# Scores of the samples' paged keys: half of the pages as one product on VectorE and sums on ScalarE

## The chip, the cores and the metric

The kernel runs on one core of a Trainium2 chip. The metric is device time in microseconds, the median of several executions. The engines named below are PE (TensorE, matrix products), VectorE (DVE), ScalarE (ACT), GpSimd (POOL) and SyncE (SP), whose queue issues the transfers (DMA). "The profile" is one recorded execution.

## The reference

One inference step of a decoder trunk with two layers, for a prompt of 512 tokens and 8 samples of one token each. Layer 0 runs a convolution module and a stick-breaking attention of 8 heads of width 128 side by side behind one input projection; layer 1 is a gated DeltaNet. All is fp32. The change touches one thing, the logits of a sample's query against its past of 2048 keys, which lie in 16 pages of 128 keys (drawn by `page_table` from a pool of 160 pages):

```python
k_past = cache_k[j][page_table].reshape(n_seq, past_len, SB_HEADS, SB_HEAD_DIM)
z = jnp.einsum('bqhd,bkhd->bhqk', q.astype(F32), k.astype(F32)) * (SB_HEAD_DIM ** -0.5)
z = z + bias.astype(F32)[None, :, None, None]
```

From z follow softplus, a reversed cumulative sum over the keys, the weights, and their sum over the pages of values.

## The kernel before, in words

Tokens lie on the free dimension (512 + 8 = 520 columns), features on the 128 partitions. A projection takes a weight block of 8 x 128 x 128 from HBM (`weights`), ScalarE casts it to a high part `wh`, VectorE subtracts to get the low part `wl`, and PE adds three products of high and low parts into a PSUM tile `pg` (`products`); `wr` has three buffers, `wh` and `wl` two each.

Layer 0 goes over the 8 heads. Head h has the projections of convolution group h (`conv_gemm`), of k and v, and of two gates; then 31 taps of the depthwise convolution on one accumulator tile `acc` (`conv_taps`; the first on ScalarE, 30 on VectorE), a group norm (`conv_norm`, whose result is stored to HBM), the work of the samples, and the prompt's attention (`prompt_attention`, with exponentials and logarithms on ScalarE). The samples' work is spread over the heads: `scores(b)` of samples 0 and 1 at head 0, of 2, 3, then 4 and 5 at head 3, then 6 at head 4 and 7 at head 5, and `mix(b - 1)`, which multiplies the pages of values, beside them.

`scores(b)` copies the sample's query, spread over all partitions, to `qbc` (128 x 8 heads x 128). For each of the 16 pages it loads the page of keys (128 keys x 8 heads x 128, 512 KB) into a tile `page` (`page`, line 838 on); there are five such slots, which pages of values and other tiles use too. For each head one VectorE instruction multiplies the page's 128 columns by `qbc` and sums them into one column of z (`accum_out`), which the hardware runs as the product and a read of the accumulator.

Nothing runs in the order of the program's text. Each operation is recorded (`record`) with an engine, a cost, and a priority, its place in the text plus a bias; `flush` plans all of layer 0 as a list schedule with these costs, and each engine then gets its instructions in the planned order, which it keeps. Weight blocks have a bias far ahead of all, the matrix products one far behind, and `scores` and `mix` stand 2000 places ahead. By the written costs a score product takes 1.04 x 128 + 68 + 12 = 213 ns on VectorE, a product of 1024 columns 1.04 x 1024 + 68 = 1133 ns, and an accumulating ScalarE copy of 128 columns 0.83 x 128 + 109 + 105 = 320 ns. As every operation is issued from one helper, the profile gives line 431 for nearly all; groups are told apart by their tiles.

Of the kernel before, what the change touches and what calls it, by code (L numbers as in the profile page):

```python
# [11 lines left out]
AF = mybir.ActivationFunctionType  # L12
ALU = mybir.AluOpType
# [11 lines left out]
H = 8  # L25
# [471 lines left out]
def build(tc, a, ctx):  # L497
    nc = tc.nc
    sc = Sched(tc)
    V, S, G, PE, Q = (sc.engine(e) for e in ("DVE", "ACT", "POOL", "PE", "SP"))  # L500
# [17 lines left out]
    def C(name, p=P):  # L518
        o, n = COFF[name]
        t, lo, _ = next(x for x in tabs if x[1] <= o < x[2])  # L520
        return t[:p, o - lo:o - lo + n]
# [149 lines left out]
    with ExitStack() as l0:  # L671
# [165 lines left out]
        def page(b, p, cache):  # L837
            kt = pgp.tile([P, H, P], F32, name="page")
            sel = ptab[0:1, b * NPG + p:b * NPG + p + 1]

            def load():
                r = nc.sync.value_load(sel, min_val=0, max_val=NPOOL - 1)
                nc.sync.dma_start(kt, cache[bass.ds(r, 1)].rearrange("o p h d -> (o p) h d"))
            sc.record("SP", "page", load, (), {}, out=[kt], ins=[sel], cost=(340, 4 * P * P * H))
            return kt

        def scores(b):

            qbc = lp.tile([P, H, P], F32, name="qbc", bufs=1)
            for g in range(2):  # L850
                qp = pm.tile([P, 4, P], F32, name="pd", bufs=1)
                PE.matmul(qp.rearrange("p j d -> p (j d)"), sel8[:, b:b + 1].broadcast_to([P, P]),
                          qrow[:, g * 4:g * 4 + 4, :].rearrange("p j d -> p (j d)"), start=True, stop=True)
                S.copy(qbc[:, g * 4:g * 4 + 4, :], qp)
            z = lp.tile([P, H, NPG], F32, name="dz", bufs=2)
            for p in range(NPG):
                kt = page(b, p, a["cache_k"])
                for h in range(H):
                    junk = lp.tile([P, P], F32, name="junk", bufs=4)
                    V.scalar_tensor_tensor(junk, kt[:, h, :], 1.0, qbc[:, h, :], op0=ALU.mult, op1=ALU.mult,  # L860
                                           accum_out=z[:, h, p:p + 1])
            V.scalar_tensor_tensor(z, z, ISQ, sbb[:, :, None].broadcast_to([P, H, NPG]), op0=ALU.mult, op1=ALU.add)
            e = lp.tile([P, H, NPG], F32, name="de")
            w = lp.tile([P, H, NPG], F32, name="dw")
            S.activation(e, z, AF.Abs)
            S.activation(e, e, AF.Exp, scale=-1.0)
            V.tensor_scalar(w, e, 1.0, None, op0=ALU.add)
            V.scalar_tensor_tensor(e, w, 1.0, e, op0=ALU.subtract, op1=ALU.subtract)
            S.activation(w, w, AF.Ln)
            V.tensor_tensor(w, w, e, op=ALU.subtract)  # L870
            V.scalar_tensor_tensor(w, z, 0.0, w, op0=ALU.max, op1=ALU.add)
            wf = w.rearrange("p h g -> p (h g)")
            p1 = pm.tile([P, 2, P], F32, name="pd", bufs=1)
            PE.matmul(p1[:, 0, :], C("tri"), wf, start=True, stop=True)
            PE.matmul(p1[:, 1, :], ones, wf, start=True, stop=True)
            tot = lp.tile([P, H, NPG + 1], F32, name="dtot")
            V.memset(tot[:, :, NPG:], 0.0)
            V.tensor_copy(tot[:, :, 0:NPG], p1[:, 1, :].rearrange("p (h g) -> p h g", h=H))
            suf = lp.tile([P, H, NPG + 1], F32, name="dsuf")
            V.tensor_tensor_scan(suf.rearrange("p h g -> p (h g)")[:, ::-1], C("scan_dec")[:, ::-1],  # L880
                                 tot.rearrange("p h g -> p (h g)")[:, ::-1], 0.0, op0=ALU.mult, op1=ALU.add)
            V.tensor_tensor(z, z, suf[:, :, 1:], op=ALU.subtract)
            V.tensor_tensor(z, z, p1[:, 0, :].rearrange("p (h g) -> p h g", h=H), op=ALU.subtract)
            return z
# [26 lines left out]
        def head_gemm(h):  # L911
            ps = gemm1(8 + 3 * h)
            kt = lp.tile([P, NT], F32, name="kq", bufs=2)
            S.copy(_pn(kt), ps)
            Q.dma_start(a["o_k"][h], kt)
            ps = gemm1(8 + 3 * h + 1)
            vt = lp.tile([P, NT], F32, name="vt", bufs=2)
            S.copy(_pn(vt), ps)
            Q.dma_start(a["o_v"][h], vt)
            return kt, vt  # L920
# [65 lines left out]
        for h in range(H):  # L986
            with sc.prio(-HP):
                gp, win = conv_gemm(h)
                kt, vt = head_gemm(h)
                az, gate = gates_gemm(h)  # L990
            acc = conv_taps(h, gp, win)
            conv_norm(h, acc, az)
            with sc.prio(-2000):
                for b in ((0, 1), (2,), (3,), (4, 5), (6,), (7,), (8,), ())[h]:
                    z_next = scores(b) if b < NB else None
                    if b:
                        mix(b - 1, z_last)
                    z_last = z_next
            prompt_attention(h, kt, vt, gate)
            if h in (2, 3, 5, 6):  # L1000
                ada(0, 8 + (2, 3, 5, 6).index(h), lp)
# [119 lines left out]
    with ExitStack() as es:  # L1121
        op = sc.pool(es, "out0", 2)
# [699 lines left out]
    with ExitStack() as es:  # L1822
        op = sc.pool(es, "out1", 2)
# [117 lines left out]
```

## Time and profile before

| | |
|---|---|
| median of 3 runs | 3222.65 us (3216.93 to 3229.28) |
| profiled execution | 3229.8 us, span 3228.0 us |
| PE busy | 3072.7 us, 95% |
| VectorE busy | 2346.4 us, 73% |
| ScalarE busy | 1578.2 us, 49% |
| GpSimd busy | 128.3 us, 4% |
| mean granted clock of TensorE | 0.965 |

Busy times are sums over the span of an engine's records. Matmuls are pipelined and their ends are modelled, so a busy PE is not PE at its peak; records of VectorE and ScalarE overlap those of the next instruction, so the distance between starts is the better price of one. A wait is put down to the releaser that came last.

### The profile page before, as it was taken

What the parts mean: (1) busy time and instruction counts of PE and PEld (TensorE: products, weight loads), DVE (VectorE), ACT (ScalarE), POOL (GpSimd) and SP (SyncE); (2) the same over time, 40 slices, a digit from 0 to 9 for tenths busy, and PEclk for the clock granted to TensorE, in tenths of its full rate; (3) what the DMA queues carried; (4) which work ended last, traced back from release to release, by engine and by line L of the source; (5) the groups of instructions that cost most, each with busy time, mean ns of one, the idle gap of its engine ahead of it and who ended that gap; (6) DMA issues with size and microseconds to landing.
All of it is one profiled execution on the core that took longest, in us unless ns stands there. A gap on an engine that the chain in (4) does not pass through costs nothing.

```text
span 3228.0 us, 65519 instructions
## 1 busy us (share of the span) xinstructions
PE 3072.7 (95%) x24448; PEld 2800.0 (87%) x24448; DVE 2346.4 (73%) x6470; ACT 1578.2 (49%) x2942; POOL 128.3 (4%) x157
## 2 busy tenths in 40 slices
PE   8999999998979999999999979999999989999997
PEld 5798888886868886998999969999989779989997
DVE  3477988789674476676999749999956566665755
ACT  3234344433543366777773236555535555554544
POOL 0000000000001111000000000000000000001111
PEclk9999999999979999999999989999989789899998
DMA  9988898989627798687664485555364444476754
GB/s 316 296 274 292 298 313 293 327 306 316 219 89 260 287 308 276 141 168 149 151 155 135 110 153 176 154 150 168 127 180 146 137 126 154 130 247 193 227 181 137
DMA packets 361586, 667.01 MB, mean 207 GB/s; under 512 B 103698, under 2 KB 216339, under 8 KB 357171
## 3 DMA queue, kind: packets, MB, share of 16 engines
q1 hardware_dynamic: 361266, 662.82, 67.4%
q8 instruction: 192, 3.15, 0.4%
q14 instruction: 128, 1.04, 0.1%
HBM read 574.95 MB, written 87.70 MB: 205 GB/s over the span
## 4 chain that ended last, share of the span: by engine, by line
PE 84%; DVE 7%; DMA 6%; ACT 1%; SPq 1%; issue 1%; POOLq 0%; ACTq 0%; POOL 0%; DVEq 0%
PE pg L431 66%; PE pm L431 9%; PE pl L431 6%; PE pd L431 2%; SPq L431 1%; DVE wl L431 1%; DVE junk L431 1%; DMA S<-state_delta 1%; DMA page<-cache_k 1%; DMA wa<-w_ada 1%; DVE blk L431 1%; DVE acc L431 1%; DVE S L431 1%; DMA o_ds<-S 1%; DMA m<-sp 0%
## 5 line engine op out<-in xcount | busy, mean ns | idle before, releaser
L431 PE MATMUL pg<-uh,wh 128*128 128x260 f32 (+1 forms) x6112 | 1343.3, 290 | 12.5 <-ACT wh L431 6.2
L431 PE MATMUL pg<-ul,wh 128*128 128x260 f32 (+1 forms) x6112 | 1344.0, 289 | 3.0 <-DVE ul L431 2.6
L431 PEld LDWEIGHTS pg<-uh,wh 128*128 128x128 f32 (+1 forms) x6112 | 1001.0, 191 | 67.1 <-issue 46.0
L431 PEld LDWEIGHTS pg<-ul,wh 128*128 128x128 f32 (+1 forms) x6112 | 1004.0, 191 | 46.0 <-issue 33.8
L431 ACT CAST wh<-wr 128x1024 fp32r<-128x1024 f32 (+3 forms) x508 | 512.5, 1010 | 769.0 <-PE pg L431 634.2
L431 PE MATMUL pg<-uh,wl 128*128 128x260 f32 (+1 forms) x6112 | 880.6, 287 | 0.2
L431 DVE TENSOR_TENSOR wl<-wr,wh 128x1024 fp32r<-128x1024 f32 (+3 forms) x508 | 616.0, 1213 | 328.1 <-ACT wh L431 145.6
L431 PEld LDWEIGHTS pg<-uh,wl 128*128 128x128 f32 (+1 forms) x6112 | 791.6, 190 | 42.4 <-issue 37.3
L431 DVE SCALAR_TENSOR_TENSOR junk<-page,qbc 128x128 f32<-128x128 f32 x1024 | 223.2, 293 | 7.7 <-DMA page<-cache_k 4.4
L431 DVE TENSOR_TENSOR tmp<-m 128x224 f32<-128x224 f32 (+19 forms) x238 | 200.8, 844 | 4.0
L431 DVE SCALAR_TENSOR_TENSOR acc<-gp,conv_w_a,acc 128x512 f32<-128x512 f32 x240 | 181.5, 756 | 4.1 <-ACT acc L431 1.1
L431 ACT ACT_TABLE_LOAD x123 | 157.8, 1283 | 22.5 <-DVE rs L431 10.9
L431 DVE SCALAR_TENSOR_TENSOR cacc<-buf,conv_w_c,cacc 128x512 f32<-128x512 f32 x192 | 143.2, 746 | 13.8 <-ACT cacc L431 12.0
L431 DVE TENSOR_REDUCE m<-tmp 128x32 f32<-128x224 f32 (+19 forms) x238 | 131.1, 551 | 4.0
L431 DVE DVE_READ_ACCUMULATOR junk<-page,qbc 128x1 f32 x1024 | 90.2, 88 | 0.0
L431 PE MATMUL pl<-page,wst 128*32 128x512 f32 x512 | 80.2, 611 | 8.8 <-DMA page<-cache_v 8.8
L431 PE MATMUL pl<-wa,cpad 128*32 128x512 f32 x512 | 82.9, 604 | 2.7 <-DMA wa<-w_ada 2.7
L431 PE MATMUL pg<-yh,wh 128*128 128x260 f32 x320 | 79.2, 284 | 0.7 <-ACT wh L431 0.7
L431 PE MATMUL pg<-yl,wh 128*128 128x260 f32 x320 | 78.9, 283 | 0.0
L431 DVE SCALAR_TENSOR_TENSOR S<-S,egb,pl 128x128 f32<-128x128 f32 x256 | 71.9, 341 | 5.7 <-PE pl L431 5.2
L431 ACT ACTIVATE jk<-osb 128x128 f32<-128x128 f32 x128 | 39.7, 310 | 54.9 <-DVE osb L431 53.9
L430 ACT ACT_TABLE_LOAD x51 | 65.4, 1283 | 0.9
(381 smaller groups left out, 3418.8 us busy)
## 6 DMA issues: line engine op xcount, KB each, us to landing
wr<-w_in_odd SPq DMA_DIRECT2D x194, 512.0 KB, 4.6
page<-cache_k SPq DMA_DIRECT2D x128, 512.0 KB, 5.5
wa<-w_ada SPq DMA_DIRECT2D x128, 512.0 KB, 5.4
page<-cache_v SPq DMA_DIRECT2D x128, 512.0 KB, 5.7
wr<-w_out_odd SPq DMA_DIRECT2D x128, 512.0 KB, 3.7
wr<-w_in_even SPq DMA_DIRECT2D x94, 512.0 KB, 5.5
page<-w_ada SPq DMA_DIRECT2D x128, 256.0 KB, 5.0
pk<-sp SPq DMA_DIRECT2D x64, 448.0 KB, 4.0
```

Of the source, the lines that this page charges most:

```text
L430: self.tc.nc.scalar.preload_act_table_set("natural_log_exp_and_others")
L431: o[2](*o[3], **o[4])
```

## The change

For odd pages VectorE multiplies the whole page in place by `qbc`, one instruction of 1024 columns. ScalarE then copies each head's 128 columns onto themselves with an accumulator, whose sum goes to the same column of z as before. Even pages stay as they were. The page's slot is free when the last copy is done. The planner orders the layer anew with the new operations.

```diff
--- before.py
+++ after.py
@@ -855,6 +855,11 @@
             z = lp.tile([P, H, NPG], F32, name="dz", bufs=2)
             for p in range(NPG):
                 kt = page(b, p, a["cache_k"])
+                if p % 2:
+                    V.tensor_tensor(kt, kt, qbc, op=ALU.mult)
+                    for h in range(H):
+                        S.activation(kt[:, h, :], kt[:, h, :], AF.Copy, accum_out=z[:, h, p:p + 1])
+                    continue
                 for h in range(H):
                     junk = lp.tile([P, P], F32, name="junk", bufs=4)
                     V.scalar_tensor_tensor(junk, kt[:, h, :], 1.0, qbc[:, h, :], op0=ALU.mult, op1=ALU.mult,
```

## Rows read from the trace of the kernel before

**Rows 1.** Stretches of layer 0: busy us (instructions) per engine, granted clock, DMA share, GB/s.
```profile
360.00:480.00 120.00, 119.00 (x933) 99.48 (x932) 107.38 (x404) 48.60 (x73) 2.21 (x4) 1.00 0.93 311
...
720.00:760.00 40.00, 40.00 (x319) 37.08 (x319) 27.97 (x190) 17.33 (x27) 0.96 (x1) 1.00 0.89 293
760.00:800.00 40.00, 29.52 (x181) 15.30 (x180) 39.65 (x146) 10.99 (x20) 1.07 (x1) 0.91 0.93 338
...
880.00:960.00 80.00, 57.61 (x417) 54.70 (x416) 58.11 (x109) 41.24 (x67) 3.12 (x3) 0.81 0.31 93
```

**Rows 2.** Chain of waits from 150 to 1000 us, shares by line.
```profile
by line: PE pg L431 60.9%; PE pl L431 9.9%; PE pm L431 9.0%; DVE junk L431 3.5%; DMA page<-cache_k 2.8%; DVE acc L431 2.0%; DVE wl L431 1.8%; PE pd L431 1.5%; DVE E L431 1.0%; DMA page<-cache_v 1.0%; DVE W L431 0.9%; DMA wa<-w_ada 0.8%; DMA
```

**Rows 3.** VectorE in order of time: start, us, instruction, count, idle before it.
```profile
643.96 0.69 DVE L431 TENSOR_TENSOR gp<-pg,sg 128x512 f32<-128x512 f32 x1
...
771.05 0.76 DVE L431 SCALAR_TENSOR_TENSOR acc<-gp,conv_w_a,acc 128x512 f32<-128x512 f32 x1
...
868.24 0.68 DVE L431 TENSOR_TENSOR gp<-pg,sg 128x512 f32<-128x512 f32 x1
...
887.16 0.41 DVE L431 TENSOR_REDUCE acc<-wm 128x8 f32<-128x248 f32 x1 [5.76 <-DMA yd<-acc]
...
890.36 0.75 DVE L431 SCALAR_TENSOR_TENSOR acc<-gp,conv_w_a,acc 128x512 f32<-128x512 f32 x1
```

**Rows 4.** PE in order of time: its waits, 768 to 959 us.
```profile
768.08 3.66 PE L431 MATMUL pl<-page,wst 128*32 128x512 f32 x8 [6.08 <-DMA page<-cache_v]
...
930.49 2.07 PE L431 MATMUL pm<-acc,avg 128*128 128x260 f32 x4 [4.16 <-DVE acc L431]
...
958.38 0.47 PE L431 MATMUL pm<-ct,Z 128*128 128x128 f32 x1 [12.77 <-DVE Z L431]
```

**Rows 5.** Score products: duration ns min/median/max; VectorE idle before them, us, times.
```profile
L431 DVE SCALAR_TENSOR_TENSOR junk<-page,qbc x1024: 278/292/918, 179.3 to 769.8; 128x128 f32<-128x128 f32 x171
L431 DVE DVE_READ_ACCUMULATOR junk<-page,qbc x1024: 74/88/103, 179.5 to 770.0; 128x1 f32 x171
...
  DMA page<-cache_k: 4.4, 4
```

**Rows 6.** VectorE in order of time, 409 to 414 us.
```profile
409.61 0.29 DVE L431 SCALAR_TENSOR_TENSOR junk<-page,qbc 128x128 f32<-128x128 f32 x1
...
412.16 0.29 DVE L431 SCALAR_TENSOR_TENSOR junk<-page,qbc 128x128 f32<-128x128 f32 x1
...
412.37 1.23 DVE L431 TENSOR_TENSOR wl<-wr,wh 128x1024 fp32r<-128x1024 f32 x1
413.51 0.29 DVE L431 SCALAR_TENSOR_TENSOR junk<-page,qbc 128x128 f32<-128x128 f32 x1
```

**Rows 7.** ScalarE in order of time, layer 1.
```profile
2033.80 0.31 ACT L431 ACTIVATE jk<-osb 128x128 f32<-128x128 f32 x1
2034.01 0.19 ACT L431 ACTIVATION_READ_ACCUMULATOR jk<-osb 128x1 f32 x1
2034.10 0.36 ACT L431 CAST dm<-pd 128x256 fp32r<-128x256 f32 x1
```

**Rows 8.** ScalarE groups: busy us, mean ns of one, idle before.
```profile
L431 ACT CAST wh<-wr 128x1024 fp32r<-128x1024 f32 x464 | 487.1, 1050 | 722.1 <-PE pg L431 598.6 <-issue 39.1 <-DVE junk L431 38.1
...
L431 ACT ACTIVATE jk<-osb 128x128 f32<-128x128 f32 x128 | 39.7, 310 | 54.9 <-DVE osb L431 53.9
...
L431 ACT ACTIVATION_READ_ACCUMULATOR jk<-osb 128x1 f32 x128 | 24.1, 188 | 0.0
```

**Rows 9.** Waits of SP queue, 180 to 780 us: total us, times, longest.
```profile
SPq L431 <- DVE junk L431: 83.6, 50, 6.4
SPq L843 <- DVE junk L431: 64.0, 117, 4.2
```

**Rows 10.** Waits of ScalarE, 180 to 780 us: total us, times, longest.
```profile
ACT wh L431 <- PE pg L431: 166.3, 50, 6.9
```

**Rows 11.** DMA issues: count, KB each, median us from issue to landing.
```profile
page<-cache_k SPq DMA_DIRECT2D x128, 512.0 KB, 5.5
```

## Prediction, made before the result was known

> **What bounds the kernel now.** I read the stages first, since the scores stand in one of them: from about 180 to 770 us of the span, in layer 0 [rows 1]. There PE, as far as the profile marks it busy, is full (119.00 of 120 us between 360 and 480), VectorE nearly so (107.38 of 120) and ScalarE at 48.60 of 120. [...]
>
> [...] The planner puts the scores 2000 places ahead, so VectorE does the convolution taps and the attention of the heads when the scores leave it time. Head 5's glu product is written at 643.96, but its run of taps begins at 771.05, when the last sample's products are over: 127 us late. Heads 6 and 7 follow on the one accumulator tile; head 7's input is ready at 868.24, its tile is free only when the store of head 6 has landed (VectorE's idle of 5.76 us before 887.16), and its taps begin at 890.36 [rows 3]. The PE waits that this makes are a few: 6.08 us at 768.08 for pages of values, 4.16 us at 930.49 for the taps, 12.77 us at 958.38 for head 7's attention [rows 4], 23.0 us together. That is what a lighter VectorE can win back, not VectorE's busy time.
>
> **The change part by part.** 8 samples of 16 pages have 64 odd pages. On each, 8 score products with their accumulator reads go from VectorE, one product of 1024 columns comes, and 8 copies with accumulation come to ScalarE.
>
> VectorE, removed: the records are 292 ns for the product and 88 ns for the read, 1024 of each [rows 5], but they overlap: from 409.61 to 412.37 there are 13 products, 0.212 us apart [rows 6]. A page is 8 x 0.212 = 1.70 us. Added: the nearest row is the subtraction of a weight block, also two fp32 operands of 1024 columns: its record is 1.23 us, the next instruction starts 1.14 us behind its start [rows 6]. I take 1.14, a saving of 0.56 us per odd page and 64 x 0.56 = 36 us in all; by the whole record 0.47 and 30 us; if the reads did not overlap at all, 8 x 0.380 - 1.23 = 1.81 and 116 us, which the rows exclude.
>
> ScalarE, added: the nearest instruction is the sum of squares in layer 1, 128 columns with an accumulator. Its record is 0.31 us and the read's 0.19 [rows 7, 8], but the next instruction starts 0.30 us behind the start [rows 7]. So 512 copies are 154 us by the spacing and 512 x 0.50 = 256 us by the records; I take 154. ScalarE was busy 48.60 of 120 us, 40% [rows 1]; over 590 us that makes 236 + 154 = 390 us, 66%, or 83% by the upper end. It does not become the bound as a sum.
>
> [...]
>
> What the copies stand in front of: ScalarE issues in order, and behind a copy that waits for its product stand the casts of weight blocks, for which PE waits, the evacuations of PSUM and the exponentials of attention. Cover: ScalarE waited 166.3 us in 50 waits for PE to hand back a cast buffer, 3.3 us each [rows 10], more than 8 x 0.30 = 2.4 us; with two buffers a cast that is 2.4 us late does not reach PE. Without that cover each odd page costs up to 2.4 us, 154 us in all; I take nothing and keep a small part of it as a rival.
>
> The page slot: five slots hold pages of keys and of values. A page of keys was read in 1.70 us; an odd one is held 1.14 + 2.4 = 3.5 us, 1.8 us more (3.4 by the records). A page needs 5.5 us from issue to landing [rows 11], and SP, whose queue is in order, already waits 64.0 us at the page loads and 83.6 us at its other transfers for score products [rows 9]. Yet VectorE waited only 4.4 us for pages of keys [rows 5]: they were there. So I take nothing here; if the slots were the limit it costs 64 x 1.8 / 5 = 23 us, at the upper end 44. The number and bytes of the transfers stay.
>
> The sum: behind 770 us the chain of taps starts earlier by the last sample's 8 x 0.56 = 4.5 us. Of the 31 us saved on the other 56 odd pages VectorE passes on what it had queued: with 11% idle between 360 and 480 the queue was not always full, and the attention steps wait for ScalarE and PE as well; I take a third, 10 us. Against it 3 us, for attention's steps on ScalarE that stand behind a page's copies. The chain moves 12 us forward, and the tail can use it, since the 4.16 and 12.77 us of PE's waits lie there; next late is PE's own stream of projections. On the profiled execution (3229.8 us, its span 3228.0 with 1.8 around it) that gives 3217.8; this execution is 7 us over the median of the runs, 3222.65, so I forecast 3222.65 - 12 = 3211, with 3199 to 3222 as its own range (23 us down, all the PE waits named, or nothing won). The whole order of layer 0 is planned anew from the costs written in the kernel (1.70 us for an old page, 1.13 for the product, 8 x 0.32 on ScalarE), so each engine's sequence shifts. I bound that by the 12 us of the effect itself, either way.
>
> **The rivals.**
> 1. Nothing to see: PE is the bound until its projections are through and the tail's latency is head 7's own, conv norm and attention one behind the other. For it: 119.00 of 120 us of PE, and only 3.5% of score products on the chain. Against it: taps 127 us behind their input. The same holds if the product on the chip takes as long as what it replaces. Time 3222.
> 2. All of it arrives: the 36 us come through whole where VectorE is 89% busy, the wait at 768.08 goes too, and with fewer stops the clock stays up. Against it: only 23.0 us of PE waits are in sight, so the rest would have to come from the low clock between 880 and 960. 30 us off: 3193.
> 3. Slower, by the slots: an odd page leaves its slot 1.8 us later, the next load in SP's queue waits, and weight blocks behind it too. For it: 147.6 us of SP's waits for score products. Against: pages were there before VectorE wanted them. It decides from the point at which VectorE's wait for pages of keys grows from 4.4 us to tens. 23 us: 3246.
> 4. Slower, by ScalarE's order: a copy that waits for its product holds a weight cast back for longer than the two buffers cover. If each odd page costs PE 0.5 us, 32 us: 3255.
>
> **How the numbers follow.** Chances: forecast 0.45, rival 1 0.20, rival 2 0.18, rival 3 0.12, rival 4 0.05. About 0.5%, 16 us, is what a measurement of this kernel can tell from no change. Below 3206.5 lie rival 2 and a third of the forecast: 0.18 + 0.15 = 0.33. Within: 0.30 + 0.20 = 0.50. Above 3238.8: 0.12 + 0.05 = 0.17. The range that should hold 8 in 10 goes down past rival 2 to 3186 and up to rival 3 at 3246; outside lie a part of rival 2 with the larger gains, half of rival 3 and rival 4.
>
> **What the changed profile would show.** Right: 64 products of 1024 columns with the next start 1.1 to 1.2 us behind; 512 left of the old products; 512 copies of 0.3 us with reads of 0.19; VectorE 30 to 36 us less by spacing (its busy total falls further, as the records of products overlap); taps of heads 5 to 7 earlier, and PE's wait for head 7's attention earlier by about as much as the time falls. The cover of the casts holds if PE's waits for cast blocks stay near zero; the slots don't bind if VectorE's wait for pages of keys stays in single microseconds. Wrong: a first tap of head 7 that is no earlier, PE waiting for weight blocks in the stage, SP waiting for ScalarE at page loads for more than the 64.0 us that it waited for VectorE, or a shift of the same size in layer 1, where nothing of the change is.

## The result, and the profile after

The changed kernel takes 3189.0 us (median of 4 runs, 3179.07 to 3194.78) beside 3221.59 for the kernel before (4 runs), a ratio of 0.9893 with an interval of 0.9858 to 0.9929. The forecast was 3211, and the measured 33 us less is the size of rival 2, which had 3193. A second measurement, e5 below, gave 0.9874.

The operations came as priced. First the changed kernel's instructions of the score pages: durations min/median/max in ns, first and last start; the last line is VectorE's idle before them, us and times.

```profile
L431 ACT ACTIVATE page<-page x512: 292/295/317, 197.5 to 816.9; 128x128 f32<-128x128 f32 x171
L431 ACT ACTIVATION_READ_ACCUMULATOR page<-page x512: 185/187/197, 197.7 to 817.1; 128x1 f32 x171
...
L431 DVE TENSOR_TENSOR page<-page,qbc x64: 1207/1218/1628, 195.8 to 811.6; 128x1024 f32<-128x1024 f32 x64
...
  DMA page<-cache_k: 13.7, 14
```

The old products that are left:

```profile
L431 DVE SCALAR_TENSOR_TENSOR junk<-page,qbc x512: 248/285/294, 180.4 to 811.4; 128x128 f32<-128x128 f32 x171
```

And the spacing in order of time (start, us, instruction). VectorE:

```profile
199.79 1.22 DVE L431 TENSOR_TENSOR page<-page,qbc 128x1024 f32<-128x1024 f32 x1
200.93 0.28 DVE L431 SCALAR_TENSOR_TENSOR junk<-page,qbc 128x128 f32<-128x128 f32 x1
```

ScalarE:

```profile
198.06 0.29 ACT L431 ACTIVATE page<-page 128x128 f32<-128x128 f32 x1
198.26 0.18 ACT L431 ACTIVATION_READ_ACCUMULATOR page<-page 128x1 f32 x1
198.35 0.29 ACT L431 ACTIVATE page<-page 128x128 f32<-128x128 f32 x1
```

A product takes 1.14 us to the next start, as the subtraction it was priced by [rows 6]; a copy with its read takes 0.29 [rows 7 had 0.30]. VectorE's wait for pages of keys went from 4.4 to 13.7 us [rows 5], so the slots stand tighter, beyond the single microseconds that the prediction took as the sign that they don't bind; e10 asks whether that costs anything.

The waits of SP's queue and of ScalarE between 180 and 780 us (total us, times, longest):

```profile
SPq L431 <- DVE junk L431: 60.8, 31, 4.9
...
SPq L843 <- DVE junk L431: 17.1, 12, 4.2
...
SPq L843 <- ACT page L431: 6.0, 8, 1.8
```

```profile
ACT wh L431 <- PE pg L431: 39.2, 20, 5.8
ACT page L431 <- DVE page L431: 32.4, 21, 3.0
```

SP waits less for score products than before [rows 9], and 6.0 us for ScalarE's copies at the page loads. ScalarE waits for cast buffers 39.2 us where it was 166.3 [rows 10]: the copies fill its idle time. 32.4 us are copies that wait for their product.

The stretches that answer to [rows 1], in the changed kernel:

```profile
360.00:480.00 120.00, 118.92 (x951) 104.81 (x951) 94.83 (x289) 83.90 (x264) 2.89 (x4) 1.00 0.90 302
...
720.00:760.00 40.00, 39.76 (x311) 33.69 (x310) 25.14 (x84) 32.58 (x95) 0.96 (x2) 1.00 0.96 322
760.00:800.00 40.00, 40.00 (x326) 36.88 (x326) 39.32 (x143) 26.64 (x95) 0.76 (x1) 1.00 0.83 286
...
880.00:960.00 80.00, 72.55 (x523) 58.43 (x521) 46.56 (x109) 41.46 (x76) 1.45 (x2) 0.94 0.68 234
```

Up to 770 us PE gains little; it was full. But the stop after 760 is gone (40.00 of 40 us against 29.52), and between 880 and 960 PE is busy 72.55 us instead of 57.61, at a mean granted clock of 0.94 instead of 0.81. The end of the layer as one stretch, before:

```profile
770.00:1000.00 230.00, 201.39 (x1475) 165.30 (x1473) 162.70 (x312) 106.36 (x170) 6.70 (x8) 0.91 0.57 193
```

and after:

```profile
770.00:1000.00 230.00, 221.73 (x1675) 181.78 (x1667) 149.30 (x383) 115.66 (x283) 4.14 (x5) 0.98 0.79 268
```

20.3 us more of PE work in the same 230 us, with the clock at 0.98 where it was 0.91. What VectorE does there is seen in the lines that answer to [rows 3]:

```profile
640.28 0.68 DVE L431 TENSOR_TENSOR gp<-pg,sg 128x512 f32<-128x512 f32 x1
...
666.44 0.74 DVE L431 SCALAR_TENSOR_TENSOR acc<-gp,conv_w_a,acc 128x512 f32<-128x512 f32 x1
...
833.32 0.68 DVE L431 TENSOR_TENSOR gp<-pg,sg 128x512 f32<-128x512 f32 x1
...
853.22 0.74 DVE L431 SCALAR_TENSOR_TENSOR acc<-gp,conv_w_a,acc 128x512 f32<-128x512 f32 x1
```

Head 5's taps begin 26 us behind their input (640.28 to 666.44) instead of 127, head 7's input comes 35 us earlier and its taps at 853.22 instead of 890.36, 37 us earlier. PE's wait for head 7's attention shrinks from 12.77 us [rows 4] to this:

```profile
925.82 0.47 PE L431 MATMUL pm<-ct,Z 128*128 128x128 f32 x1 [3.75 <-DVE Z L431]
```

How much of the two profiled executions' difference belongs to the change is seen at the first instruction behind layer 0's attention, the first residual sum (first and last start are behind the durations). Before:

```profile
L431 DVE SCALAR_TENSOR_TENSOR blk<-blk,hx x22: 689/694/1807, 994.3 to 3183.2; 128x520 f32<-128x520 f32 x22
```

after:

```profile
L431 DVE SCALAR_TENSOR_TENSOR blk<-blk,hx x22: 689/693/1802, 962.9 to 3137.1; 128x520 f32<-128x520 f32 x22
```

994.3 against 962.9: 31.4 us are won by then. The spans differ by 46.1 us, but from there on the engines' sequences are the same in both programs: 16991 matmuls, 3422 instructions of VectorE and 2221 of ScalarE on named tiles, each engine's in one and the same order in the two profiles. From that mark to the end of the span it is 2233.7 us before and 2219.0 after; among the profiles of the experiments it lies between 2209 and 2228, so this part is put down to scatter between executions and not to the change.

What PE did up to that mark says where the 31.4 us come from. From the start of the span to the mark, busy us (instructions) of PE, PEld (its weight loads), VectorE, ScalarE and GpSimd, then the granted clock, DMA share and GB/s; before, then after:

```profile
0.00:994.30 994.30, 941.02 (x7459) 800.18 (x7460) 735.49 (x3049) 396.18 (x608) 17.10 (x30) 0.97 0.83 277
```

```profile
0.00:962.90 962.90, 934.29 (x7459) 797.75 (x7460) 701.41 (x2090) 550.55 (x1637) 17.46 (x30) 0.99 0.86 286
```

PE runs the same 7459 matmuls. Its idle time falls from 53.3 to 28.6 us, 24.7 us less, and its busy time by 6.7 us, at a clock of 0.99 instead of 0.97; together that is the 31.4 us.

Of the 37 us at head 7's first tap, 35 are already in its input, which comes from PE: from input to first tap it is 22.1 us before and 19.9 after. In the new order PE reaches head 7's projections ahead of other work. On PE the tile `pl` is written by the products with pages of values and with the weight tile `wa`. The instructions that write or read it between head 7's input and the mark, busy us (instructions) of PE, PEld, VectorE and ScalarE, then clock, DMA share and GB/s, before and after:

```profile
868.24:994.30 126.06, 2.13 (x16) 0.32 (x16) 0.00 (x0) 0.59 (x1) 0.85 0.38 114
```

```profile
833.32:962.90 129.58, 24.22 (x160) 3.64 (x160) 0.00 (x0) 2.33 (x4) 0.96 0.73 245
```

So 22 us of PE's work went behind head 7's input, where PE had stood idle.

### The profile page after: what moved, and what is told of

Same layout as the page of the kernel before. It is cut to its first block, busy times and chain, and to the rows that moved or that the text cites. A ratio compares the mean times of both kernels' runs of the same rounds, so it can differ in the third digit from the quotient of the medians.

```text
span 3181.9 us, 65555 instructions
## 1 busy us (share of the span) xinstructions
PE 3051.3 (96%) x24448; PEld 2787.3 (88%) x24448; DVE 2315.0 (73%) x5510; ACT 1729.7 (54%) x3971; POOL 131.5 (4%) x157
## 4 chain that ended last, share of the span: by engine, by line
PE 83%; DVE 6%; DMA 6%; SPq 2%; ACT 2%; issue 1%; POOLq 0%; ACTq 0%; DVEq 0%
PE pg L431 65%; PE pm L431 9%; PE pl L431 6%; SPq L431 2%; PE pd L431 2%; DVE wl L431 1%; DMA page<-cache_k 1%; DMA wa<-w_ada 1%; DMA S<-state_delta 1%; DMA page<-cache_v 1%; DVE acc L431 1%; DVE S L431 1%; DVE blk L431 1%; DVE junk L431 1%; DMA m<-sp 0%
## 5 line engine op out<-in xcount | busy, mean ns | idle before, releaser
L431 ACT ACTIVATE page<-page 128x128 f32<-128x128 f32 x512 | 151.0, 297 | 39.3 <-DVE page L431 36.8
L431 DVE SCALAR_TENSOR_TENSOR junk<-page,qbc 128x128 f32<-128x128 f32 x512 | 115.3, 285 | 13.8 <-DMA page<-cache_k 10.7
L431 ACT ACTIVATION_READ_ACCUMULATOR page<-page 128x1 f32 x512 | 96.1, 188 | 0.0
L431 DVE TENSOR_TENSOR page<-page,qbc 128x1024 f32<-128x1024 f32 x64 | 78.4, 1225 | 3.0 <-DMA page<-cache_k 3.0
L431 PE MATMUL pl<-page,wst 128*32 128x512 f32 x512 | 72.9, 604 | 0.3 <-DMA page<-cache_v 0.2
```

The source lines that it names most:

```text
L431: o[2](*o[3], **o[4])
```

## The experiments

Two theories at first. V: VectorE has 36 us less to do, and the taps and the attention that it had put off come earlier. P: the planner's new order puts the samples' work elsewhere, and PE's idle tail is filled by that. In the table the last start of a tap of head 7 and PE's idle time from the start of the span to the mark, the first residual sum (both in us, in the one profiled execution of each), stand beside the ratio to the kernel before:

| kernel | last tap | PE idle | ratio | interval |
|---|---|---|---|---|
| e12 change, no precedence | 861.3 | 25.5 | 0.9877 | 0.9845 to 0.9909 |
| e3 no sums | 881.1 | 30.2 | 0.9887 | 0.9872 to 0.9902 |
| e5 the change again | 884.2 | 27.0 | 0.9874 | 0.9840 to 0.9907 |
| the change | 890.5 | 28.6 | 0.9893 | 0.9858 to 0.9929 |
| e11 before, no precedence | 896.0 | 32.5 | 0.9877 | 0.9852 to 0.9903 |
| e6 every fourth page | 900.2 | 37.9 | 0.9907 | 0.9879 to 0.9936 |
| e10 change, six slots | 906.6 | 42.0 | 0.9931 | 0.9893 to 0.9968 |
| e1 order of the change, work of before | 913.3 | 46.5 | 0.9969 | 0.9950 to 0.9989 |
| before | 929.6 | 53.3 | 1 | |
| e2 order of before, work of the change | 934.2 | 53.4 | 1.0037 | 1.0023 to 1.0051 |
| e4 samples a head later | 944.4 | 59.8 | 1.0057 | 1.0040 to 1.0075 |
| e8 sums on VectorE | 961.2 | 77.6 | 1.0124 | 1.0090 to 1.0158 |
| e9 all pages, six slots | 1000.0 | 108.4 | 1.0213 | 1.0184 to 1.0241 |
| e7 all pages | 1018.9 | 110.6 | 1.0277 | 1.0244 to 1.0310 |

**e1 and e2, order and work crossed.** The planner's order and the instructions were exchanged: in e1 the planner gets the changed kernel's operations, but each odd page's product issues the 8 old score products and the 8 copies issue nothing; in e2 it gets the operations of before, but the first of 8 issues the product of 1024 columns, the last the 8 copies, the others nothing. PE's and SP's sequences are those of the kernel whose order it is.

The edit of e1, against the changed kernel:

```diff
-                    V.tensor_tensor(kt, kt, qbc, op=ALU.mult)
+                    def eight(kt=kt, p=p):
+                        for h in range(H):
+                            nc.vector.scalar_tensor_tensor(kt[:, h, :], kt[:, h, :], 1.0, qbc[:, h, :], op0=ALU.mult,
+                                                           op1=ALU.mult, accum_out=z[:, h, p:p + 1])
+                    sc.record("DVE", "tensor_tensor", eight, (), {}, out=[kt, z[:, :, p]], ins=[kt, qbc],
+                              cost=(1.04 * H * P + 68, True))
                     for h in range(H):
-                        S.activation(kt[:, h, :], kt[:, h, :], AF.Copy, accum_out=z[:, h, p:p + 1])
+                        sc.record("ACT", "activation", lambda: None, (), {}, out=[kt[:, h, :], z[:, h, p:p + 1]],
+                                  ins=[kt[:, h, :]], cost=(0.83 * P + 109 + 105, AF.Copy))
```

The edit of e2, against the kernel before:

```diff
                     junk = lp.tile([P, P], F32, name="junk", bufs=4)
+                    if p % 2:
+                        def part(h=h, kt=kt, p=p):
+                            if h == 0:
+                                nc.vector.tensor_tensor(kt, kt, qbc, op=ALU.mult)
+                            if h == H - 1:
+                                for j in range(H):
+                                    nc.scalar.activation(kt[:, j, :], kt[:, j, :], AF.Copy, accum_out=z[:, j, p:p + 1])
+                        sc.record("DVE", "scalar_tensor_tensor", part, (), {}, out=[junk, z[:, h, p:p + 1]],
+                                  ins=[kt[:, h, :], qbc[:, h, :]], cost=(1.04 * P + 80, True))
+                        continue
```

> Work as before (8 score products with accumulator reads per odd page on VectorE, nothing on ScalarE), but issued in the order that the planner gives the changed kernel; PE's and SP's sequences are the changed kernel's. Theory V (the gain is VectorE's lighter work, 36 us, passed on to the taps and the attention): no gain without the work, 3215 to 3230. Theory P (the gain is the new order: the samples' pages and their PE work fall later, into PE's idle tail): most of it, 3185 to 3200.

> Work as in the changed kernel (one product per odd page on VectorE, 8 accumulating copies on ScalarE), issued in the order planned for the kernel before; PE's and SP's sequences are those before. Theory V: 3185 to 3200. Theory P: 3215 to 3230, or slower, since copies that were not planned stand in ScalarE's queue.

Measured: e1 0.9969, e2 1.0037; both together, the change, 0.9893 and 0.9874. On 3213 us that is 10 us down, 12 us up, and some 34 to 40 down. e2 came out as theory P had it; e1, at 3202.65 us, lies between the two, so neither theory holds as a whole. The work alone under the old order wins nothing. (How much of e2's 12 us is lost to copies that stand unplanned in ScalarE's queue was not separated.) In e2, VectorE is busy 35 us less between 180 and 770 us, yet the end of the layer is as before:

```profile
770.00:1000.00 230.00, 200.02 (x1448) 163.56 (x1449) 163.86 (x318) 109.17 (x190) 6.41 (x8) 0.89 0.57 193
```

and PE waits in the same places, for attention's Z (14.8 us before) and for pages of values (8.8 before), between 180 and 1000 us (total us, times, longest):

```profile
PE pm L431 <- DVE Z L431: 14.7, 3, 12.8
PE pl L431 <- DMA page<-cache_v: 10.4, 6, 5.7
```

Each engine keeps its planned sequence, as the two profiles of before and after do behind the mark, and PE, whose sequence is that of before, does not reach head 7's input sooner (872.94 us, before 868.24). In e1 the order is there, but VectorE is too slow for it: between 180 and 770 us PE is busy 568.32 of 590 us, in the changed kernel 583.41. A quarter to a third of the gain is left. Last taps of e1, then of e2:

```profile
L431 DVE SCALAR_TENSOR_TENSOR acc<-gp,conv_w_a,acc x240: 723/749/1137, 205.7 to 913.3; 128x512 f32<-128x512 f32 x120
```

```profile
L431 DVE SCALAR_TENSOR_TENSOR acc<-gp,conv_w_a,acc x240: 723/748/1100, 214.5 to 934.2; 128x512 f32<-128x512 f32 x120
```

What wins in the change is an order planned for a lighter VectorE together with the work that lets it be kept.

**e3, are the copies a cost?** In the changed kernel the 8 accumulating copies became one copy of 8 columns, so the odd pages' scores are left out.

```diff
-                    for h in range(H):
-                        S.activation(kt[:, h, :], kt[:, h, :], AF.Copy, accum_out=z[:, h, p:p + 1])
+                    S.copy(z[:, :, p], kt[:, :, 0])
```

> Changed kernel whose ScalarE sums are left out: for odd pages one small copy of the first column of each head's product goes to z in their place, so ScalarE has 64 small copies and not 512. Theory V: as fast as the changed kernel or faster, 3175 to 3190, since ScalarE's 151 us are only a cost. Theory P: slower than the changed kernel, 3195 to 3215, since the samples' work runs earlier again.

0.9887, within the interval of the change: ScalarE's 512 copies, with the order planned for them, cost nothing that can be measured. The order is another one here: the step behind the last sample's scores starts at 766.9 us, nearly as early as before (770.9), where the change has 817.5, and only 7.80 us of work in `pl` lie between head 7's input (847.8) and the mark, where the change has 24.22. The gain is the same, so theory P is not needed for it.

**e4, the samples moved by hand** in the kernel before, its work otherwise untouched.

```diff
-                for b in ((0, 1), (2,), (3,), (4, 5), (6,), (7,), (8,), ())[h]:
+                for b in ((0,), (1,), (2,), (3,), (4, 5), (6,), (7,), (8,))[h]:
```

> Kernel before with the samples spread differently over the heads: one sample less at head 0, so that scores of samples 1, 2, 3 come a head later, 4 and 5 at head 4 and so on, and the last sample's values are mixed at head 7. Scores as before, on VectorE alone. Theory V: VectorE has the same work, no gain, 3215 to 3230. Theory P: the samples' PE work falls into PE's idle tail, 3190 to 3205.

1.0057, slower than either theory had it: the scores, still with their precedence, now stand ahead of the taps and the attention of the last heads, and head 7's last tap comes at 944.4. PE has 13.29 us of work in `pl` behind head 7's input, 11 us more than before, and is idle for longer all the same (59.8 us): later samples in PE's idle tail are not enough to win.

**e5 to e8, the dose.** e5 is the changed kernel, measured again. e6 takes every fourth page, e7 every page, and e8 sums on VectorE, each against the changed kernel. e6:

```diff
-                if p % 2:
+                if p % 4 == 3:
```

e7:

```diff
-                if p % 2:
+                if True:
```

e8:

```diff
-                    for h in range(H):
-                        S.activation(kt[:, h, :], kt[:, h, :], AF.Copy, accum_out=z[:, h, p:p + 1])
+                    V.tensor_reduce(z[:, :, p:p + 1].rearrange("p h o -> p (h o)"), kt, op=ALU.add, axis=AX.X)
```

> The changed kernel once more, beside the others. 0.986 to 0.993 of the kernel before.

> The change on every fourth page instead of every second: VectorE relieved of 18 us instead of 36, ScalarE with 256 copies, order planned for it. Theory V2 (the gain is planned VectorE time): about half of the change's gain, 0.993 to 0.996 of before. Rival L (each new order falls out differently by chance, up to 1% either way): anything between 0.985 and 1.01.

> The change on all pages: VectorE relieved of 72 us, ScalarE with 1024 copies, 302 us more than before. Theory V2 without a limit: twice the gain, 0.979. With the limits seen: PE idle in layer 0 is nearly used up by the change, and ScalarE would be at nine tenths while the scores run, so 0.985 to 1.00. Rival L: anything between 0.985 and 1.01.

> Odd pages as one product and one reduction of 8 x 128 columns on VectorE, nothing on ScalarE: fewer instructions than before, but about 1.14 + 1.13 = 2.27 us instead of 1.70 us per odd page, 36 us more VectorE time, planned so. Theory V2: slower by about what the change gained, 1.007 to 1.013 of before. Rival L: anything between 0.985 and 1.01, no tie to the sign. If fewer instructions are what counts: 0.99.

e8 is the mirror of the change: by the estimate 36 us more of VectorE (records of 1.23 us for each of 64 products and 1.22 for each of 64 reductions), planned so, 1.0124, and the last tap 32 us later. In e5, e6 and e8 the sign follows VectorE's planned time; in e7 it does not. Last taps of e8:

```profile
L431 DVE SCALAR_TENSOR_TENSOR acc<-gp,conv_w_a,acc x240: 723/751/1316, 232.1 to 961.2; 128x512 f32<-128x512 f32 x120
```

e6, with half the relief, has 0.9907, some three quarters of the gain and more than was expected of half the relief; its interval overlaps those of the change, so that the gain levels off is a reading and not shown. e7 is 1.0277, worse than its expectation. ScalarE is at 104.38 of 120 us, as expected, and VectorE has fallen to 81.41, yet PE stops:

```profile
360.00:480.00 120.00, 105.88 (x843) 95.49 (x841) 81.41 (x107) 104.38 (x494) 0.97 (x2) 0.95 0.85 275
```

VectorE's wait for pages of keys is the 51.8 us that rival 3 asked for, and PE waits for pages of values:

```profile
  DMA page<-cache_k: 51.8, 38
```

```profile
PE pl L431 <- DMA page<-cache_v: 48.6, 22, 13.5
```

**e9 and e10, six page slots** in e7 and in the changed kernel, to tell slots from ScalarE.

```diff
-        pgp = sc.pool(l0, "pages", 5)
+        pgp = sc.pool(l0, "pages", 6)
```

> The change on all pages, with six page slots instead of five. Theory slots (in the kernel with all pages the five slots are held by ScalarE's copies, so that pages come late and the weight blocks behind them): most of the loss goes, 0.99 to 1.01 of before. Theory ScalarE (its 302 us of copies are too much while the scores run): the loss stays, 1.02 to 1.03.

> The changed kernel with six page slots instead of five. If slots held longer cost the change anything: 0.975 to 0.984 of before. If they don't: 0.985 to 0.990, as the change.

e9 1.0213: a sixth slot gives back a small part, and VectorE still waits 50.4 us for keys. At the page loads SP waits for ScalarE's copies 69.9 us, and 64.9 in e7 (180 to 1000 us). That the rest of the loss is ScalarE's load is the candidate left, argued from this and from its 104.38 of 120 us and not isolated; whether more slots would go on giving was not tried. e10 0.9931, outside both of its expectations: no better than the change, if anything worse, although VectorE's wait for keys falls from 13.7 to 4.9 us. So no price of the slots is seen in the change. But the planner orders the layer anew for six slots too (the last copy starts at 769.9 us instead of 816.9), so neither run shows the slot by itself.

**e11 and e12, the order alone.** The precedence around the samples' work was dropped, in the kernel before (e11) and in the changed one (e12).

```diff
-            with sc.prio(-2000):
+            with sc.prio(0):
```

> Kernel before with the samples' work planned in the place of the text, without its lead of 2000 places; VectorE's work as before. If what counts is only that taps and attention are served earlier on VectorE: 0.985 to 0.995 of before. If VectorE's total time is what counts, serving one before the other wins nothing: 0.997 to 1.01.

> The changed kernel with the samples' work planned in the place of the text, as in the run before: the two gains together. If both draw on the same idle time of PE in layer 0: 0.983 to 0.989 of before, hardly better than either. If they add: 0.974 to 0.978.

e11: 0.9877, the whole gain of the change, with VectorE's work as it was. So the gain does not need a lighter VectorE; an order does it. Which part of the order, the runs do not isolate: head 5's taps begin at 665.8 us, soon after their input (632.5), but 23.40 us of PE's work in `pl` also lie behind head 7's input, as in the change. e3 has the gain with little of the second (7.80 us), e4 some of the second without the gain, so the earlier taps are the likelier part. The end of the layer in e11:

```profile
770.00:1000.00 230.00, 213.44 (x1621) 174.53 (x1614) 153.95 (x506) 92.87 (x152) 4.09 (x5) 0.96 0.78 267
```

Last taps of e11, then of e12:

```profile
L431 DVE SCALAR_TENSOR_TENSOR acc<-gp,conv_w_a,acc x240: 725/748/1120, 194.2 to 896.0; 128x512 f32<-128x512 f32 x120
```

```profile
L431 DVE SCALAR_TENSOR_TENSOR acc<-gp,conv_w_a,acc x240: 726/750/1219, 195.1 to 861.3; 128x512 f32<-128x512 f32 x120
```

e12 has its last tap 35 us before e11's and the same ratio, 0.9877: the two gains do not add. The ratio no longer follows the last tap below about 900 us. What it goes with over the whole table is PE's idle time up to the mark: of the 25.5 to 32.5 us that the five fastest rows have left, some 14 lie before 180 us in each of the profiles, ahead of the scores. The mark itself comes at 947.0 us in e12's profile and at 961.5 in e11's, a difference that the ratios do not show. No version is shown to beat the change.

## Why the prediction was right in direction and too small

- Prices: right. 1.14 us for a product and 0.29 to 0.30 for a copy, so 36 us saved and 148 to 154 added. By e3 (0.9887, the change 0.9893) these copies, with the order planned for them, cost the kernel nothing that can be measured.
- What binds: right in part. The end of the layer does hang on head 7's taps and attention: over the fourteen profiles the ratio rises with the last tap of head 7 from about 900 us on. But head 7 was as late behind its input after the change (19.9 us) as before (22.1). What moved was the input, 35 us, and that is PE's stream, which the prediction named only as "next late" and left where it was in the sum.
- The step that failed is the sum's "I take a third, 10 us" with the bound on the replanned order, "the 12 us of the effect itself". Measured: 37 us at head 7's first tap and 31.4 us at the end of layer 0. The gain came by way of the order: without it, e2, the same 36 us saved on VectorE came with a loss of 12, and with another order and nothing saved, e11, the whole gain is there. So it is a coincidence that the gain is about as large as the saving, as rival 2 had it.
- The cap of 23.0 us from three waits of PE was too low. In 770 to 1000 us PE was busy 201.39 of 230 us, so 28.6 us were idle, and the clock stood at 0.91; the change recovers 20.3 us of idle time there, and the clock rises to 0.98. The two stretches in [rows 1], 760 to 800 and 880 to 960 us, already show 32.9 us without work on PE, and the sum did not use them.
- The 3189.0 lies outside the forecast's own range (3199 to 3222) and 3 us inside the wide one (3186 to 3246), which reached so far down for rival 2. That it holds the result is in part luck, since neither the forecast nor rival 2 has the gain come from the order.
- The casts' cover: nothing speaks against it. e3, which has hardly any copies, is no faster, and among PE's waits in the changed kernel (180 to 1000 us) none is for `wh` or `wl`, the parts of a weight block. The slots, rival 3: no price seen in the change (e10), and at most a small part of the loss in the kernel with all pages (e9), with the reserve that both have another order. Rival 4 did not come.
- "A shift of the same size in layer 1" was named as a sign of being wrong. The two profiles show 14.7 us there; it is put down to scatter, since the sequences are the same and the other twelve profiles spread over 19 us.

Open: why the planner with a lighter VectorE finds an order that serves taps earlier, rather than one that finishes the scores earlier, was not followed through its decisions. e6 and e8 show that here the gain and the loss had the sign of VectorE's relief or load, not that they must; e7 has the opposite sign. So rival L of these runs, that each new order falls out well or badly by chance, is not excluded.

## What to carry to other kernels

Where each engine keeps an order planned ahead, time taken off an engine can be worth nothing until the order is planned for it, as in e2 (35 us less of VectorE, 1.0037): cross order and work before crediting either. Look at the last consumer of the crowded engine, here head 7's taps, at what stands in front of it, and at when its input comes; and add up the idle time of the engine that has the most work, here PE, up to the end of the stage. A change of precedence can give the same as moving work (e11 0.9877, the change 0.9893), and the two need not add (e12 0.9877). And more of the same can turn a gain into a loss: half the pages won a hundredth, all pages lost nearly three.

## What the runs showed of the hardware

An accumulating ScalarE copy of 128 columns is spaced by 0.29 us although its two records add to 0.48, and 13 VectorE products with accumulator reads by 0.212 each although theirs add to 0.38: the read's record overlaps that of the next instruction. Two executions of the same sequences in layer 1 differ by as much as 25 us (2209 to 2234 from the mark to the end), a difference that a comparison of two profiles should not put down to a change.
